# Second FFN products: a fifth tile by quarters in the second half of the columns, and another order of its tiles

## The chip, the cores and the metric

The kernel runs on one core of a Trainium2 chip. The metric is the time of one execution on the device in microseconds (us), the median of several runs. TensorE (PE) multiplies, VectorE (DVE), ScalarE (ACT) and GpSimd (POOL) prepare operands and take results away, and SyncE (SP) issues the transfers from the chip's main memory. Each engine works through its own list of instructions in order.

## What is computed

One decoder layer on 512 tokens of width 1024 in float32: a feed-forward network (FFN), a token mixer and a second FFN, each with a norm before and after it and a residual sum.

```python
def swiglu_ffn(x, w_in, w_out):
    gate, up = jnp.split(x @ w_in, 2, axis=-1)
    return (jax.nn.silu(gate) * up) @ w_out          # (512,1024) @ (1024,5632), then (512,2816) @ (2816,1024)

x = x + 0.5 * rms_norm(swiglu_ffn(rms_norm(x, g0), w_in1, w_out1), p0)
x = x + rms_norm(token_mixer(rms_norm(x, g1), ...), p1)
x = x + 0.5 * rms_norm(swiglu_ffn(rms_norm(x, g2), w_in2, w_out2), p2)
```

The change concerns the second product of both FFNs, h @ w_out, with h the gated 512 x 2816 array.

## The kernel before

**Split operands.** Every operand of a large product is kept as two arrays: a high part (ACT copies the value into TensorE's fast 32-bit format, lines 273 and 812) and a low part, the rest (DVE subtracts, lines 275 and 813). A product of two tiles is then three products: high by high, high by low, low by high.

**The second product by tiles.** `ffn_out` (line 858) works in two halves of the 1024 output columns. In each half it adds up 11 tiles; a tile (its number is called k2 in the code) is 256 of the 2816 inner positions. `OUT` (line 83) is the order of the tiles in each half. A whole tile (`plain`, line 886) takes 48 matrix multiplications of 128 x 256 (line 893). A tile by quarters (`quartered`, line 906) uses a scheme of Winograd's kind with seven instead of eight block products, and takes 42 (line 901). `QUARTERED` (line 82) names the tiles by quarters: six in the first half, four in the second. Their common results are put together once per half (`common`, lines 925 to 929) and added to the sums (`add`, line 934, its operations on line 863).

**What a tile by quarters needs beside that.** Its weights are split twice: three quarters as they are (128 x 768), and then, after four sums in place in the loaded buffer (`sum_quarters`, line 306), all four quarters (128 x 1024). On the side of h there are the quarters as they are (`h_quarters`, line 822, three of four) and four sums (`h_sums`, line 837, on DVE's line 844), which `s_tile` splits. The sums of h stay in place in `hf` if the tile is quartered in the second half too (`stay`), and the quarters are kept (`kept`) until then. Otherwise the sums go to a buffer of their own (`hsum`).

**Buffers.** Split weights have four places (`WBUF`), split h has three places under the tag "s" (`s_place`); two of the three hold tiles 9 and 10 (`AGAIN`) from the end of the first half until they are used in the second. `PLACES` and `LATER` put some parts of h into four buffers `xq` of the FFN's input that are free by then. Quarters with no place there go into "raw" buffers (named `once`), the ring of three through which weights of the first product and of the mixer are loaded. Weights of w_out are loaded by SP through the ring "raw2" of five buffers, in the order of `OUT`. The buffer "gpre" holds the gain of the norm before each part (line 152).

**The last four tiles of the second half** (`LAST`) are done in another order: their weights and h are all prepared, and `chunk` (line 984) goes through the four groups of 128 tokens, so that the first group's norm and residual sum start while the others are multiplied. `post1` (lines 485 and 493) does this, with the root taken on POOL (line 442).

**What follows the first FFN.** `head4` (line 548) starts the mixer's first four products (`head_mm`, line 543) while the norms of the last two groups of tokens are still made: `scaled` (line 465) writes the normed rows, `trans` turns them on TensorE (line 348).

**Order of work.** The source is written in the wished order. A scheduler that runs at build time, with an estimate of each instruction's duration, sets the order in which each engine's list is written, and when a buffer of a ring is handed on. Nothing is reordered at run time.

Of the kernel before, what the change touches and what calls it, by code (L numbers as in the profile page):

```python
# [9 lines left out]
F32R = mybir.dt.float32r  # L10
AF = mybir.ActivationFunctionType
ALU = mybir.AluOpType
PSUM = bass.MemoryType.PSUM

P = 128
T = 512
D = 1024
# [5 lines left out]
RAW, WBUF, PAD, LATE, NEXT, FRONT, STEP = 3, 4, 128, 112, 64, 96, 16  # L23
PAIRS = NF // 2
# [54 lines left out]

QUARTERED = [(2, 3, 4, 6, 7, 8), (2, 4, 6, 8)]
OUT = [list(range(PAIRS)), [9, 2, 4, 10, 6, 8, 0, 1, 3, 5, 7]]
LAST = 4
PLACES, LATER = {2: 1, 4: 2, 6: 0, 8: 3}, {0: (1, 0), 7: (2, 3)}

AGAIN, ROWS = (9, 10), (18, 19, 20, 21)

# [27 lines left out]
class Layer:  # L116
# [705 lines left out]
    def h_quarters(self, k2, n=None):  # L822

        src = self.by_chunk(k2)
        parts = self.x_place(n) if n is not None else [
            self.wp.tile([P, D], F32R, tag="raw", bufs=RAW, name=self.nm("once"))[:, P - 2 * STEP :] for _ in range(2)
        ]
        parts = [v[:, : 3 * QUARTER].rearrange("p (k c t) -> p k c t", c=2, t=P) for v in parts]
        self.two_parts(*(v[:, 0] for v in parts), src[:, 0, 1])
        self.two_parts(*(v[:, 1:] for v in parts), src[:, 1])  # L830
        return [[None] + [v[:, j] for j in range(3)] for v in parts]
# [5 lines left out]
    def h_sums(self, k2, stay):  # L837

        a = self.by_chunk(k2)
        f = self.hf[:, 2 * k2 : 2 * k2 + 2, :]  # L840
        if not stay:
            f = self.sp.tile([P, 2, T], F32, tag="xn", bufs=1, name=self.nm("hsum"))
        v = f.rearrange("p k (c u t) -> p k u c t", u=2, t=P)
        tt = lambda out, x, y, op: self.nc.vector.tensor_tensor(out, x, y, op=op)
        tt(v[:, 0, 0], a[:, 0, 1], a[:, 0, 0], ALU.subtract)
        tt(v[:, 1, 0], v[:, 0, 0], a[:, 1, 0], ALU.add)
        for k in range(2):
            tt(v[:, k, 1], a[:, k, 1], v[:, 1, 0], ALU.subtract)
        return f

    def s_tile(self, f):
# [6 lines left out]
    def ffn_out(self, gpost_row, scale, after, trans, head):  # L858
# [4 lines left out]
        tt = lambda out, a, b, op: nc.vector.tensor_tensor(out, a, b, op=op)  # L863
        seq = [(half, k2) for half in range(2) for k2 in OUT[half]]
        made = deque((h, None) for h in self.hs)
# [3 lines left out]
        def more(n):  # L869
            while count[0] < min(n, len(seq)):  # L870
                half, k2 = seq[count[0]]
                count[0] += 1
                if k2 in QUARTERED[half]:
                    if k2 not in kept:
                        stay = k2 in QUARTERED[1]
                        kept[k2] = self.h_quarters(k2, PLACES.get(k2)), self.h_sums(k2, stay)
                    a, f = kept[k2]
                    made.append((a, self.s_tile(f)))
                elif half and k2 in AGAIN:
                    made.append(again.popleft())  # L880
                else:
                    made.append((self.h_tile(k2, self.x_place(*LATER[k2]) if half and k2 in LATER else None), None))
                    if not half and k2 in AGAIN:
                        again.append(made[-1])
# [47 lines left out]
        def add(C, T, u):  # L932
            for v in range(2):
                tt(C[u][v], C[u][v], T[u, v], ALU.add)
# [9 lines left out]
        for half in range(2):  # L944
            C = [[self.ps() for _ in range(2)] for _ in range(2)]
            M, T, left = None, None, len(QUARTERED[half])
            for m, k2 in enumerate(OUT[half][: PAIRS - LAST * half]):
                more(n + 2)
# [9 lines left out]
                else:  # L958
                    w = self.pull()
                    more(len(seq) if half and m == PAIRS - LAST - 1 else n + 3)  # L960
                    for i in (0, 2, 1, 3):
# [13 lines left out]
        ws = []  # L975
        for k2 in OUT[1][-LAST:]:
            ws.append(self.pull())
            more(n + 1)
            n += 1
        hs = [made.popleft()[0] for _ in range(LAST)]  # L980

        add(C, T, 1)

        def chunk(i):
            vn = [(v, n) for v in range(2) for n in range(LAST)]
            if i == 0:

                vn.sort(key=lambda f: f[1])
            for v, n in vn:
                plain(C, ws[n], hs[n], i, v, False)  # L990
                if v and i == NT - 1:
                    self.drop(ws[n])
                if v and n == LAST - 1 and i == 0:
                    add(C, T, 0)
                if n == LAST - 1:
                    yield 2 - v
# [78 lines left out]
    def ffn_items(self, name, w_in, w_out):  # L1075
# [47 lines left out]
        for h in range(2):  # L1123
            for k2 in OUT[h]:
                src = w_out[k2 * 2 * P : (k2 + 1) * 2 * P, h * 512 : (h + 1) * 512].rearrange("(k p) d -> p k d", p=P)
                key = (name, "out", h, k2)
                made.append(Item(key, [Load(key, src, 2, 512, "raw2", 5, 8)], sums=k2 in QUARTERED[h]))
                if k2 in QUARTERED[h]:
                    made.append(Item(key, ()))
# [699 lines left out]
```

## Time and profile before

| | |
|---|---|
| median of 3 runs | 936.55 us (936.34 to 937.08) |
| the profiled execution | 936.35 us, its span 934.6 us, granted TensorE clock 0.998 |
| busy in the span | PE 926.2 us, weight loads 891.8, DVE 772.1, ACT 511.4, POOL 106.5 |
| second product of the first FFN | from 224.04 us to about 341.7 us |
| second product of the second FFN | from 812.82 us to the end |

Span is the time from the first to the last instruction; 1.75 us of the execution lie outside it. In a row of the timeline stand the start, the length of a run of like instructions, the engine, the line, the operation with output and inputs, and the count. In a group's row stand the count, the busy time and the mean duration of one. The granted clock is that which the chip gave TensorE, as a share of full speed.

### The profile page before, as it was taken

The page shows a single profiled execution, that of the slowest core. Times are in us where ns is not written, and L with a number is a line of the kernel's source. Part 1 is how long each engine was busy: PE and PEld are TensorE (multiplying, and loading weights), DVE is VectorE, ACT ScalarE, POOL GpSimd, SP SyncE. Part 2 cuts the span into 40 slices and gives each one's busy share as a digit, 9 for nine tenths or more (in the row PEclk, how much of TensorE's full clock was granted, in tenths as well). Part 3 has the DMA queues.
Part 4 walks back from the last instruction along what each step waited for, and adds up shares of the span by engine and source line. Part 5 has one row for each costly group of instructions (what it writes and reads, how often), then busy time and mean ns, then how long its engine had stood idle before and what let it go on. Part 6 is the DMA issues. An engine that isn't in the chain of part 4 may idle for free.

```text
span 934.6 us, 18052 instructions
## 1 busy us (share of the span) xinstructions
PE 926.2 (99%) x7471; PEld 891.8 (95%) x7471; DVE 772.1 (83%) x1044; ACT 511.4 (55%) x735; POOL 106.5 (11%) x172
## 2 busy tenths in 40 slices
PE   9999999999999999999999999999999999999997
PEld 7999999999999999998887887899999999999997
DVE  6899988889988877698766565799899889998884
ACT  7645454557456466956533445595454545655541
POOL 3530000000001045200010310313000000000101
PEclk9999999999999999999999999999999999999999
DMA  9253343332352025421212124352354435334212
GB/s 313 94 157 91 119 132 113 93 112 71 114 177 91 24 72 134 114 70 54 81 46 69 46 91 150 98 181 70 112 158 136 136 116 159 111 91 126 79 46 91
DMA packets 86956, 101.35 MB, mean 108 GB/s; under 512 B 4277, under 2 KB 66777, under 8 KB 86874
## 3 DMA queue, kind: packets, MB, share of 16 engines
q1 hardware_dynamic: 86586, 99.68, 34.9%
q8 instruction: 58, 0.95, 0.4%
q10 hardware_dynamic: 288, 0.52, 0.2%
q14 instruction: 24, 0.20, 0.1%
HBM read 98.10 MB, written 2.10 MB: 107 GB/s over the span
## 4 chain that ended last, share of the span: by engine, by line
PE 62%; ACT 1%; issue 0%; DVE 0%; POOL 0%; DVEq 0%; POOLq 0%; ACTq 0%
PE ps L603 22%; PE ps L893 7%; PE ps L533 6%; PE ps L901 5%; PE ps L179 5%; PE ps L181 5%; PE ps L180 5%; PE ps L1307 2%; PE ps L348 1%; PE ps L543 1%; PE ps L1488 0%; PE ps L1399 0%; PE ps L1600 0%; PE ps L1573 0%; PE ps L1353 0%; PE ps L1597 0%
## 5 line engine op out<-in xcount | busy, mean ns | idle before, releaser
L273 ACT CAST w<-raw 128x1024 fp32r<-128x1024 f32 (+1 forms) x238 | 244.4, 1035 | 231.7 <-PE ps L603 92.8
L275 DVE TENSOR_TENSOR w<-raw,w 128x1024 fp32r<-128x1024 f32 (+1 forms) x238 | 290.9, 1229 | 38.0 <-ACT w L273 37.5
L603 PE MATMUL ps<-xq,w 128*128 128x256 f32 x2016 | 237.1, 277 | 0.0
L603 PEld LDWEIGHTS ps<-xq,w 128*128 128x128 f32 x2016 | 232.9, 188 | 0.0
L603 PE MATMUL ps<-sq,w 128*128 128x256 f32 x1512 | 178.0, 276 | 0.3
L603 PEld LDWEIGHTS ps<-sq,w 128*128 128x128 f32 x1512 | 174.3, 188 | 1.1 <-ACT ps L654 0.9
L893 PE MATMUL ps<-w,hs 128*128 128x256 f32 x960 | 113.0, 276 | 0.0
L893 PEld LDWEIGHTS ps<-w,hs 128*128 128x128 f32 x960 | 110.7, 188 | 0.0
L289 DVE TENSOR_TENSOR raw<-raw,raw 128x1024 f32<-128x1024 f32 x72 | 89.8, 1251 | 8.3 <-DMA raw<-in_ffn_w_in_dram 6.7
L179 PE MATMUL ps<-w,xq 128*128 128x512 f32 x192 | 78.0, 407 | 0.1
L180 PE MATMUL ps<-w,xq 128*128 128x512 f32 x192 | 74.9, 391 | 0.0
L181 PE MATMUL ps<-w,xq 128*128 128x512 f32 x192 | 74.9, 392 | 0.0
L438 POOL TENSOR_SCALAR col<-col 128x1 f32<-128x1 f32 x24 | 8.3, 347 | 513.4 <-ACT junk L437 513.3
L901 PE MATMUL ps<-w,hs 128*128 128x256 f32 x480 | 57.7, 276 | 0.0
L901 PEld LDWEIGHTS ps<-w,hs 128*128 128x128 f32 x480 | 55.9, 188 | 0.0
L533 PE MATMUL ps<-xq,w 128*128 128x256 f32 x480 | 55.7, 278 | 0.0
L533 PEld LDWEIGHTS ps<-xq,w 128*128 128x128 f32 x480 | 54.9, 188 | 0.5 <-issue 0.5
L179 PEld LDWEIGHTS ps<-w,xq 128*128 128x128 f32 x192 | 36.1, 188 | 8.5 <-issue 0.9
L181 PEld LDWEIGHTS ps<-w,xq 128*128 128x128 f32 x192 | 36.0, 188 | 8.0 <-DVE xq L355 0.3
L812 ACT CAST hs<-hf 128x1024 fp32r<-128x1024 f32 x32 | 33.7, 1052 | 17.5 <-PE ps L901 10.8
L180 PEld LDWEIGHTS ps<-w,xq 128*128 128x128 f32 x192 | 36.1, 188 | 7.3 <-DVE w L281 0.3
L813 DVE TENSOR_TENSOR hs<-hf,hs 128x1024 fp32r<-128x1024 f32 x32 | 39.0, 1217 | 1.3 <-ACT hs L812 1.2
(259 smaller groups left out, 1136.8 us busy)
## 6 DMA issues: line engine op xcount, KB each, us to landing
raw<-in_ffn_w_in_dram SPq DMA_DIRECT2D x98, 512.0 KB, 3.7
raw<-in_ffn_w_out_dram SPq DMA_DIRECT2D x44, 512.0 KB, 4.3
raw<-in_w_mix_in_dram SPq DMA_DIRECT2D x28, 512.0 KB, 3.7
raw<-in_w_mix_out_dram SPq DMA_DIRECT2D x8, 512.0 KB, 3.9
out_dram<-xs SPq DMA_DIRECT2D x8, 256.0 KB, 2.0
xs<-in_x_dram SPq DMA_DIRECT2D x6, 256.0 KB, 4.5
gpost<-in_norm_post_dram SPq DMA_DIRECT2D x3, 512.0 KB, 3.6
gpre<-in_norm_pre_dram SPq DMA_DIRECT2D x2, 512.0 KB, 4.8
```

Of the source, the lines that this page charges most:

```text
L179: mm(ps, sh, mh, start=start, stop=False, **kw)
L180: mm(ps, sh, ml, start=False, stop=False, **kw)
L181: mm(ps, sl, mh, start=False, stop=stop, **kw)
L273: nc.scalar.copy(hi, raw)
L275: self.low = nc.vector.tensor_tensor(lo, raw, hi.bitcast(F32), op=ALU.subtract)
L289: (nc.vector if late else nc.gpsimd).tensor_tensor(o, o, c, op=ALU.add)
L533: mm(ps[:, u0:u1], w[:, a, k, :], self.xop(k, b, u0, u1), start=k + n + m == 0, stop=k == ND - 1 and n == 2, skip_group_check=True,)
L603: self.nc.tensor.matmul(ps[:, c], wb[b][:, k, v], left[d][:, k, :], start=first and a + n + k == 0, stop=n == 2 and k == KH - 1, skip_grou ...
L812: self.nc.scalar.copy(hi, src)
L813: self.nc.vector.tensor_tensor(lo, src, hi.bitcast(F32), op=ALU.subtract)
L893: mm(out, a[kk][:, i * P : (i + 1) * P], w[:, b, kk, QUARTER * v : QUARTER * (v + 1)], start=begin and c == kk == n == 0, stop=kk == 1 and ...
L901: mm(ps[:, QUARTER * c : QUARTER * (c + 1)], A[a][:, c], B[b], start=begin and c == n == 0, stop=n == 2, skip_group_check=True,)
```

## The change

Tile 3 is now done by quarters in the second half too, so it keeps its quarters in two raw buffers from the first half on, and its sums of h stay in place. Tile 7, quartered in the first half alone, finds one raw buffer and puts its other quarters into the buffer "gpre". The order of the second half is 9, 2, 4, 3, 6, 8, 10 and then the last four 0, 1, 7, 5 (before: 9, 2, 4, 10, 6, 8, 0 and 1, 3, 5, 7). Tile 0 takes its place for split h under the tag "s" and no longer in `xq`. In `h_sums` the last two subtractions of 128 x 256 become one of 128 x 512 with a repeated operand; that holds for every quartered tile.

```diff
-QUARTERED = [(2, 3, 4, 6, 7, 8), (2, 4, 6, 8)]
-OUT = [list(range(PAIRS)), [9, 2, 4, 10, 6, 8, 0, 1, 3, 5, 7]]
-LAST = 4
-PLACES, LATER = {2: 1, 4: 2, 6: 0, 8: 3}, {0: (1, 0), 7: (2, 3)}
+QUARTERED = [(2, 3, 4, 6, 7, 8), (2, 3, 4, 6, 8)]
+OUT = [list(range(PAIRS)), [9, 2, 4, 3, 6, 8, 10, 0, 1, 7, 5]]
+LAST, APART = 4, 7
+PLACES, LATER = {2: 1, 4: 2, 6: 0, 8: 3}, {7: (2, 3)}
...
-        parts = self.x_place(n) if n is not None else [
-            self.wp.tile([P, D], F32R, tag="raw", bufs=RAW, name=self.nm("once"))[:, P - 2 * STEP :] for _ in range(2)
-        ]
+        once = lambda pool, tag, bufs, o: pool.tile([P, D], F32R, tag=tag, bufs=bufs, name=self.nm("once"))[:, o:]
+        if n is not None:
+            parts = self.x_place(n)
+        else:
+            places = [(self.wp, "raw", RAW, P - 2 * STEP), (self.cp, "gpre", 1, STEP // 2)]
+            parts = [once(*places[k2 == APART and m]) for m in range(2)]
...
-        for k in range(2):
-            tt(v[:, k, 1], a[:, k, 1], v[:, 1, 0], ALU.subtract)
+        tt(v[:, :, 1], a[:, :, 1], v[:, 1:2, 0].broadcast_to([P, 2, 2, P]), ALU.subtract)
```

## The prediction

> **What bounds the kernel now.** I read the busy times first, then the windows of the second half of the columns in both FFNs, then the timelines of TensorE (PE) and VectorE (DVE) there, and last the waits behind the first FFN. The page:
>
> ```profile
> span 934.6 us, 18052 instructions
> ...
> PE 926.2 (99%) x7471; PEld 891.8 (95%) x7471; DVE 772.1 (83%) x1044; ACT 511.4 (55%) x735; POOL 106.5 (11%) x172
> ...
> L893 PE MATMUL ps<-w,hs 128*128 128x256 f32 x960 | 113.0, 276 | 0.0
> ```
>
> The windows from the start of the second half to the last four tiles, 35.36 us in each FFN; the columns are the window, its length, then busy time and count of PE, weight loads, DVE, ACT, POOL, the granted clock, DMA share and GB/s:
>
> ```profile
> 282.52:317.88 35.36, 35.36 (x315) 35.36 (x313) 31.70 (x44) 21.82 (x34) 2.25 (x7) 1.00 0.23 74
> 871.30:906.66 35.36, 35.36 (x314) 35.36 (x313) 31.69 (x44) 21.80 (x34) 2.25 (x7) 1.00 0.24 74
> ```
>
> PE is busy without a gap, at full clock. DVE is busy for 31.70 of 35.36 us, so PE bounds, with 3.66 us of DVE to spare. The PE timeline of the first FFN gives the price of a multiplication:
>
> ```profile
> 271.64 16.48 PE L893 MATMUL ps<-w,hs 128*128 128x256 f32 x144
> 287.96 1.52 PE L901 MATMUL ps<-w,xq 128*128 128x256 f32 x12
> ...
> 312.44 5.60 PE L893 MATMUL ps<-w,xq 128*128 128x256 f32 x48
> ...
> 317.88 4.24 PE L893 MATMUL ps<-w,hs 128*128 128x256 f32 x36
> ```
>
> From the first row's start to the second's lie 16.32 us and 144 multiplications, so they start 16.32/144 = 0.1133 us apart. The 276 ns of the group are one's time through the array, in which others start. A whole tile is 48 x 0.1133 = 5.44 us (312.44 to 317.88), a quartered one 42 x 0.1133 = 4.76.
>
> **The change part by part.**
>
> *Fewer multiplications.* Six per FFN, twelve in all: -12 x 0.1133 = **-1.36 us**, all on the bounding engine. Whether it stays depends on the rest.
>
> *DVE in the second half of the columns.* These are its rows in the first FFN, with two of the first half's first:
>
> ```profile
> 226.44 0.41 DVE L306 TENSOR_TENSOR raw<-raw 128x256 f32<-128x256 f32 x1
> 226.78 0.41 DVE L844 TENSOR_TENSOR hf<-hf 128x256 f32<-128x256 f32 x1
> ...
> 284.22 0.94 DVE L275 TENSOR_TENSOR w<-raw,w 128x768 fp32r<-128x768 f32 x1
> 285.09 2.38 DVE L475 TENSOR_TENSOR y<-ps,gpost 128x256 f32<-128x256 f32 x6
> ...
> 290.39 2.36 DVE L275 TENSOR_TENSOR w<-raw,w 128x1024 fp32r<-128x1024 f32 x2
> ...
> 294.47 0.95 DVE L275 TENSOR_TENSOR w<-raw,w 128x768 fp32r<-128x768 f32 x1
> 295.45 1.80 DVE L306 TENSOR_TENSOR raw<-raw 128x256 f32<-128x256 f32 x4
> 298.43 2.09 DVE L275 TENSOR_TENSOR w<-raw,w 128x1024 fp32r<-128x1024 f32 x2 [1.17 <-ACT w L273]
> ...
> 304.57 1.23 DVE L275 TENSOR_TENSOR w<-raw,w 128x1024 fp32r<-128x1024 f32 x1 [1.19 <-ACT w L273]
> ...
> 318.33 1.28 DVE L863 TENSOR_TENSOR ps<-ps,hf 128x512 f32<-128x512 f32 x2
> 319.52 1.21 DVE L275 TENSOR_TENSOR w<-raw,w 128x1024 fp32r<-128x1024 f32 x1
> ```
>
> What each takes until the next may start: a split of 1024 1.14 us (2.36 - 1.22 in the pair), of 768 0.87 (284.22 to 285.09) or 0.98 if the next needs its result (294.47 to 295.45); a sum of quarters 0.34 (226.44 to 226.78) or (1.80 - 0.42)/3 = 0.46 if the next sum needs it; an add of 512 0.60. From the last sum's end (295.45 + 1.80 = 297.25) to the second split that needs it, through ScalarE's (ACT's) cast, 298.43 - 297.25 = **1.18**; the row names that wait, 1.17. I call this the handover. Tile 3 now adds per FFN one split of 768 (0.87) and four sums (4 x 0.34 = 1.34): 31.70 + 2.21 = 33.9 us of a window that shrinks to 35.36 - 0.68 = 34.68. So the sum fits, by 0.8 us; the order decides. A quartered tile costs DVE 0.98 + 4 x 0.46 + 1.14 + 1.14 = 5.1 us with its sums back to back, more than its 4.76 on PE; a whole one 2.28 against 5.44. Before, whole tile 10 stood between the quartered ones; now 2, 4, 3, 6 and 8 follow one another.
>
> I stepped through DVE's list in the new built order with these prices. PE starts tile 2 at 287.96 as before, then 4 at 292.72, 3 at 297.48, 6 at 302.24, 8 at 307.00, 10 at 311.76, the last four at 317.20. The second weights of a quartered tile are needed 18 multiplications and one more place in, at its start + 2.04 + 0.11.
> - Tile 3: first split at 291.53, three sums from 292.51, a split of h, the fourth sum at 294.91; 295.33 + 1.18 = second split at 296.51, done about 297.7. Needed 299.6.
> - Tile 6: first split 297.65, sums from 298.63 with a split of h (1.14) after the first, the last ends 301.45; tile 8's first split fills the handover; second split 302.63, done 303.8. Needed 304.4.
> - Tile 8: sums from 303.77, again with a split of h between, the last ends 306.59; tile 10's split fills the handover; second split 307.77, done 308.95. Needed 309.15: **0.2 us of spare**.
>
> So no wait there, by a hair. Then DVE makes the splits and four adds of the last four tiles. Their fourth tile, 5, finds a place for h and for weights only when tile 10 ends, at 317.20. The ACT cast of the same kind before:
>
> ```profile
> 318.08 1.05 ACT L273 CAST w<-raw 128x1024 fp32r<-128x1024 f32 x1 [4.06 <-PE ps L893]
> ```
>
> It starts 0.2 after PE's release at 317.88. Now ACT casts h at 317.4 and the weights at 318.35; DVE comes to the h of tile 5 at 319.35, behind the adds, to its weights at 320.49, done 321.6. The first group of tokens needs them 36 multiplications and one after 317.20, at 321.39. Before: 319.52 + 1.21 = 320.73 against 322.07, a spare of 1.3. I cost the difference at 0.2 to 0.3 us per FFN, **+0.6** for two. The bounds: 0 if DVE is slightly earlier than stepped; 1.2 each if one more operation of 1.14 slips ahead of it. The price lies nearest to the stepped one.
>
> [...]
>
> *Last differences of h.* One of 512 in place of two of 256, twelve times. Two take at least 2 x 0.34; one of 512, by the adds, 0.60. So each saves 0.08 or a little more, up to 1 us if all of it were on the path. But it lies beside the first product and the first half, where PE is the bound as well: I take 0. Tile 7's sums also stand earlier in DVE's list and two of tile 3's later, all still beside the first product; 0, or one sum of 0.34 at most if PE came to wait there.
>
> *Places.* Loads of w_out take:
>
> ```profile
> raw<-in_ffn_w_out_dram SPq DMA_DIRECT2D x44, 512.0 KB, 4.3
> ```
>
> Tile 7's quarters lie in the buffer of the gain until PE has used them in the first half; in the first FFN the gain's load now stands on SP's queue behind that release and behind some 18 w_out loads. Its reader is the normed row of the first group of tokens, after the last four tiles have begun: 0. Two mixer loads now wait on SP for tile 3's raw buffers, until 302.24 in the steps above; the w_out loads of tiles 7 and 5 queue behind them, land about 306.5 to 308, and have their first readers on DVE at 314.67 and 320.49 (on ACT about 1.2 earlier): 0, and up to 4.3 us if that cover of some 5 us were gone.
>
> *Behind the first FFN.* The build moves one instruction: the second group of head products is fed by two splits of mixer weights on DVE, and the normed row of the third group of tokens (line 465), which stood ahead of the last group's line 485 and 493, now stands behind them.
>
> ```profile
> 342.88 0.75 DVE L465 SCALAR_TENSOR_TENSOR xn<-xs,col,gpre 128x512 f32<-128x512 f32 x1
> 343.56 0.41 DVE L485 TENSOR_TENSOR hf<-ps,gpost 128x256 f32<-128x256 f32 x1
> 344.08 0.75 DVE L493 SCALAR_TENSOR_TENSOR xs<-y,col,xs 128x512 f32<-128x512 f32 x1
> 344.75 0.74 DVE L493 SCALAR_TENSOR_TENSOR xs<-hf,col,xs 128x512 f32<-128x512 f32 x1
> 345.41 1.22 DVE L275 TENSOR_TENSOR w<-raw,w 128x1024 fp32r<-128x1024 f32 x1
> ```
>
> What gates line 493 is GpSimd's (POOL's) root, and what follows the split is the waiting PE:
>
> ```profile
> 343.18 0.86 POOL L442 TENSOR_TENSOR col<-col,nhalf 128x1 f32<-128x1 f32 x1
> ```
>
> ```profile
> PEld ps L543 <- DVE w L275: 0.3, 1, 0.3
> ```
>
> The root ends at 344.04, line 493 starts at 344.08 and cannot start earlier; the row of 0.67 us (342.88 to 343.56) that lay in that time now comes after, so the split starts at 346.08 instead of 345.41, and PE, which waits 0.3 for it already, waits 0.67 more: **+0.67**. Bounds: 0 if the estimate of the order of arrival is off, 1.4 if both normed rows of the pair end up there.
>
> **Sum.** -1.36 + 0.6 + 0.67 = -0.1 us against the profiled execution (span 934.6 and 1.75 outside it, 936.35 us; the median of the runs, 936.55, is 0.2 above). **Forecast 936.4 us**; 0.2%, or 1.87 us, is about what a measurement can tell from no change.
>
> **Rivals.**
> 1. *The saving stays.* The last tile is in time and line 465 costs nothing: 936.55 - 1.36 = 935.2; with only one of the two, 935.8. For it: 83% of DVE's time, and a miss of the last tile by 0.2 is within my stepping's error. Against it: the wait for line 275 is there already. Chance 0.22.
> 2. *DVE is late from tile 8 on: slower.* Tile 8's second weights have 0.2 us. One handover that is not filled there (tile 10's split not ready to fill it) puts DVE 1.18 late; PE stands still 1.18 - 0.2 = 1.0 per FFN, and the last tile moves with it: -1.36 + 2 x 1.0 + 2 x 0.3 + 0.67 = +1.9, 938.4. Two such: +1.9 + 2 x 1.18 = +4.3, 940.8. It decides as soon as tile 8's second split ends after 309.15. For it: rows show both handovers of the window unfilled (1.17, 1.19). Against it: the new order has something to put in each. [...] Chance 0.24, half of it beyond 938.4.
> 3. *A multiplication's 276 ns were the price*: -12 x 0.276 = -3.3, 933.2 or, with the costs, 934.5. Against it: the 0.1133 between starts. Chance 0.04.
>
> **How the numbers follow.** My forecast, within 0.6 us, has 0.50, the three rivals 0.22, 0.24 and 0.04. The range from 935.0 to 938.5 holds the forecast, rival 1 and one handover per FFN; outside are the two-handover slip (0.13) and rival 3 (0.04). Faster by over 0.2% (below 934.7): 0.05. Slower by over 0.2% (above 938.4): 0.17. Within: 0.78.
>
> **What would show it.** Tiles 2 to 8 without a gap on PE, starts 4.76 apart; the last four from 317.20; a gap of 0.2 to 0.3 at about 321.4 that ends with line 275; a wait of the head products for line 275 of 0.9 to 1.0 instead of 0.3; the same in the second FFN, but for the head. A gap of 0.5 or more ahead of the last four, or PE's busy time unchanged, would make it wrong.

## The result, and the profile after

| | before | after |
|---|---|---|
| median | 936.61 us (6 runs, 936.05 to 937.94) | 941.08 us (6 runs, 940.33 to 941.47) |
| ratio, 95% interval | | 1.0044 (1.0032 to 1.0057) |
| the profiled execution | 936.35 us, span 934.6 | 940.33 us, span 938.2 |

The change made the kernel 4.5 us slower. The forecast was 936.4, the range ended at 938.5, and beyond that end lay only the second rival in its larger form (940.8 with two handovers lost per FFN). The profiled executions differ by 4.0 us, since the one after is the fastest of its six. Of these, 3.6 us lie in the spans; another 0.4 lies outside the span (2.13 us there instead of 1.75) and stays unexplained.

The page of the changed kernel:

```profile
span 938.2 us, 18025 instructions
...
PE 928.0 (99%) x7459; PEld 892.0 (95%) x7459; DVE 775.1 (83%) x1042; ACT 510.6 (54%) x737; POOL 104.8 (11%) x172
```

Twelve multiplications fewer, and PE busy 1.8 us longer: a share of 99% tells nothing here. The windows of the second half, from its start to the last four tiles, do:

```profile
282.63:318.62 35.99, 35.24 (x309) 34.85 (x308) 33.55 (x50) 21.95 (x36) 2.44 (x8) 1.00 0.36 103
873.32:909.32 36.00, 35.54 (x309) 35.15 (x308) 33.83 (x51) 22.09 (x36) 2.44 (x8) 1.00 0.24 74
```

They should have shrunk from 35.36 to 34.68 us and grew to 36.0. PE is no longer busy throughout. VectorE's load is what was forecast (33.55 and 33.83 against 33.9), and it is not full. TensorE's timeline shows where it waits; lines of the new kernel are two higher. First FFN:

```profile
266.74 1.52 PE L903 MATMUL ps<-w,xq 128*128 128x256 f32 x12
...
271.75 16.48 PE L895 MATMUL ps<-w,hs 128*128 128x256 f32 x144
288.07 1.52 PE L903 MATMUL ps<-w,xq 128*128 128x256 f32 x12
...
303.71 0.96 PE L903 MATMUL ps<-w,hs 128*128 128x256 f32 x7
305.40 2.21 PE L903 MATMUL ps<-w,hs 128*128 128x256 f32 x17 [0.73 <-DVE w L275]
...
309.49 3.17 PE L903 MATMUL ps<-w,hs 128*128 128x256 f32 x24
...
313.18 8.32 PE L895 MATMUL ps<-w,hs 128*128 128x256 f32 x72
```

The last quartered tile of the first half takes 271.75 - 266.74 = 5.01 us instead of 4.76: **0.25** of waiting. The five of the second half take 313.18 - 288.07 = 25.11 instead of 5 x 4.76 = 23.80: **1.31**, in tile 6 (the row at 305.40 names the second split of the weights, line 275; its 0.73 counts from the end of the multiplication before, and by the usual spacing the row was due 0.90 earlier, at 303.71 + 7 x 0.1133 = 304.50) and tile 8 (24 in 3.17 us instead of 2.88). Second FFN:

```profile
857.21 1.52 PE L903 MATMUL ps<-w,xq 128*128 128x256 f32 x12
...
862.44 16.48 PE L895 MATMUL ps<-w,hs 128*128 128x256 f32 x144
878.76 1.52 PE L903 MATMUL ps<-w,xq 128*128 128x256 f32 x12
...
895.78 2.20 PE L903 MATMUL ps<-w,hs 128*128 128x256 f32 x17 [0.42 <-DVE w L275]
...
899.86 3.26 PE L903 MATMUL ps<-w,hs 128*128 128x256 f32 x24
...
903.66 8.64 PE L895 MATMUL ps<-w,hs 128*128 128x256 f32 x72
```

The same places: 5.23 - 4.76 = **0.47**, and 24.90 - 23.80 = **1.10**. Something new stands in the last row: 72 multiplications in 8.64 us are (8.64 - 0.276)/71 = 0.1178 us apart, where the same row of the first FFN (8.32) has 0.1133. It stays so to the end of the kernel; 240 multiplications at 0.0045 us more are **1.07 us**.

Behind the first FFN, first after, then before:

```profile
342.94 4.82 PE L543 MATMUL ps<-xq,w 128*128 128x256 f32 x40
348.21 1.19 PE L543 MATMUL ps<-xq,w 128*128 128x256 f32 x8 [0.45 <-DVE w L275]
...
356.56 32.80 PE L533 MATMUL ps<-xq,w 128*128 128x256 f32 x288
```

```profile
341.76 6.13 PE L543 MATMUL ps<-xq,w 128*128 128x256 f32 x48
...
355.05 32.80 PE L533 MATMUL ps<-xq,w 128*128 128x256 f32 x288
```

From the head products to line 533 it takes 13.62 us instead of 13.29: **0.33**. From tile 10's start to the head products it takes 342.94 - 313.18 = 29.76, before (312.44 to 341.76) 29.32, for the same 240 multiplications: **0.44**, the last tile. The row of that wait and the one ahead of it:

```profile
322.70 0.28 PE L895 MATMUL ps<-w,hs 128*128 128x256 f32 x1
323.13 2.89 PE L895 MATMUL ps<-w,hs 128*128 128x256 f32 x23 [0.15 <-DVE w L275]
```

The 23 multiplications behind the wait take 2.89 us, where 22 x 0.1133 + 0.276 = 2.77; the 17 at 305.40 and at 895.78 take 2.21 and 2.20, where 16 x 0.1133 + 0.276 = 2.09. These three waits cost 0.11 to 0.12 us more than themselves, which the differences above include.

Now VectorE, in the first half. These are two second splits of weights, after:

```profile
245.34 0.42 DVE L306 TENSOR_TENSOR raw<-raw 128x256 f32<-128x256 f32 x1
246.95 2.36 DVE L275 TENSOR_TENSOR w<-raw,w 128x1024 fp32r<-128x1024 f32 x2 [1.20 <-ACT w L273]
...
251.35 1.81 DVE L306 TENSOR_TENSOR raw<-raw 128x256 f32<-128x256 f32 x4
254.35 2.09 DVE L275 TENSOR_TENSOR w<-raw,w 128x1024 fp32r<-128x1024 f32 x2 [1.20 <-ACT w L273]
...
289.03 1.80 DVE L306 TENSOR_TENSOR raw<-raw 128x256 f32<-128x256 f32 x4
```

And the same before:

```profile
245.05 0.88 DVE L306 TENSOR_TENSOR raw<-raw 128x256 f32<-128x256 f32 x2
245.85 2.43 DVE L275 TENSOR_TENSOR w<-raw,w 128x1024 fp32r<-128x1024 f32 x2
...
252.72 1.22 DVE L813 TENSOR_TENSOR hs<-hsum,hs 128x1024 fp32r<-128x1024 f32 x1
253.98 2.09 DVE L275 TENSOR_TENSOR w<-raw,w 128x1024 fp32r<-128x1024 f32 x2
...
287.38 1.79 DVE L306 TENSOR_TENSOR raw<-raw 128x256 f32<-128x256 f32 x4
```

Before, another split stood between the last sum and the second split that needs it (a whole tile's weights at 245.85, a split of h at 252.72), and VectorE went on without a pause. After, nothing stands there, and it waits 1.20 us for ScalarE's cast, at tiles 4 and 6 of each FFN. From 224 us to the half it waits 2.3 us more for such casts (6.6 instead of 4.3; some of these handovers stood open before as well) and works 0.7 us less. So it reaches the first sums of the second half (line 306) at 289.03 instead of 287.38, 1.65 us late (1.54 against TensorE, whose tile 2 starts 0.11 later), before the fifth tile has begun. The prediction started its steps from the rows of before at just this place. From there on its steps hold, moved by that lateness. It had the second splits of tiles 3 and 6 at 296.51 and 302.63; they start 1.55 and 1.49 us later:

```profile
298.06 2.09 DVE L275 TENSOR_TENSOR w<-raw,w 128x1024 fp32r<-128x1024 f32 x2 [1.17 <-ACT w L273]
...
304.12 1.23 DVE L275 TENSOR_TENSOR w<-raw,w 128x1024 fp32r<-128x1024 f32 x1 [0.25 <-ACT w L273]
```

### The profile page after: what moved, and what is told of

It reads as the page before. It is cut to its first block, busy times and chain, and to the rows that moved or that the text cites. A ratio compares the mean times of both kernels' runs of the same rounds, so it can differ in the third digit from the quotient of the medians.

```text
span 938.2 us, 18025 instructions
## 1 busy us (share of the span) xinstructions
PE 928.0 (99%) x7459; PEld 892.0 (95%) x7459; DVE 775.1 (83%) x1042; ACT 510.6 (54%) x737; POOL 104.8 (11%) x172
## 5 line engine op out<-in xcount | busy, mean ns | idle before, releaser
L895 PE MATMUL ps<-w,hs 128*128 128x256 f32 x960 | 114.4, 277 | 0.2 <-DVE w L275 0.2
L895 PEld LDWEIGHTS ps<-w,hs 128*128 128x128 f32 x960 | 111.7, 188 | 0.4 <-DVE w L275 0.4
L903 PE MATMUL ps<-w,hs 128*128 128x256 f32 x528 | 65.1, 277 | 1.4 <-DVE w L275 1.3
L903 PEld LDWEIGHTS ps<-w,hs 128*128 128x128 f32 x528 | 62.0, 188 | 2.6 <-DVE w L275 2.6
L812 ACT CAST hs<-hf 128x1024 fp32r<-128x1024 f32 x36 | 37.8, 1049 | 13.6 <-PE ps L895 8.4
L813 DVE TENSOR_TENSOR hs<-hf,hs 128x1024 fp32r<-128x1024 f32 x36 | 43.8, 1217 | 0.0
```

The source lines that it names most:

```text
L812: self.nc.scalar.copy(hi, src)
L813: self.nc.vector.tensor_tensor(lo, src, hi.bitcast(F32), op=ALU.subtract)
L895: mm(out, a[kk][:, i * P : (i + 1) * P], w[:, b, kk, QUARTER * v : QUARTER * (v + 1)], start=begin and c == kk == n == 0, stop=kk == 1 and ...
L903: mm(ps[:, QUARTER * c : QUARTER * (c + 1)], A[a][:, c], B[b], start=begin and c == n == 0, stop=n == 2, skip_group_check=True,)
```

## The experiments

Theory A: the change opened handovers in VectorE's list, so VectorE is late, and the waits are that lateness. Theory B: four more quartered tiles in a row are too much for VectorE from wherever they start. Ratios are against runs of the kernel before on the same chip.

**1. Less to do between the halves.** This version of the changed kernel leaves out four of the eight products with the gain, so its result is not the layer's.

```diff
-    def post0(self, pieces, g, scale):
+    def post0(self, pieces, g, scale, times=1):
-        y, parts = self.st("y"), []
+        y, parts = self.st("y") if times else g[:, :512], []
...
-            self.nc.vector.tensor_tensor(y[:, v], ps, g[:, v], op=ALU.mult)
+            for _ in range(times):
+                self.nc.vector.tensor_tensor(y[:, v], ps, g[:, v], op=ALU.mult)
...
-                ys = [self.post0(pieces(C, i), g, scale) for i in range(NT)]
+                ys = [self.post0(pieces(C, i), g, scale, int(i < 2)) for i in range(NT)]
```

> The changed kernel without four of the eight products with the gain between the halves (line 475, groups 2 and 3 of the tokens; the residual sum reads the gain in their place), which takes 4 x 0.39 = 1.57 us from VectorE at 283 to 289 us and leaves the rest of its list as it is. Theory A, VectorE comes out of the first half 1.65 us late and that lateness is what runs out into the waits of tiles 6 and 8: both waits (1.31 us in the first FFN, 1.10 in the second) go, 941.1 - 2.4 = 938.7 us, those of the last tile and of the first half stay. Theory B, the run of four quartered tiles after tile 2 is too much for VectorE whatever it starts from: no wait goes, 941.0 +- 0.3.

Measured: 938.59 us, ratio 1.0020 (1.0009 to 1.0031). Its first sums of the second half, in VectorE's timeline:

```profile
287.40 1.79 DVE L306 TENSOR_TENSOR raw<-raw 128x256 f32<-128x256 f32 x4
```

They stand where they stood before the change, and the waits of tiles 6 and 8 are 0.15 us in the first FFN and none in the second. That is theory A's number, and B falls: the same run of five quartered tiles runs through, but for these 0.15 us, when VectorE starts it 1.6 us earlier. The last tile still waits, 0.42 and 0.30 us.

**2. Lateness given to the kernel before** (the same switch in the kernel before, with `1 + (i > 1)` in place of `int(i < 2)`).

> The kernel before with the same four products with the gain done twice, 1.57 us more on VectorE between the halves in each FFN. Theory A: the kernel before has the spare that the changed one lacks, only the last tile's 1.3 us are overdrawn, 936.6 + 2 x (0 to 0.3), 936.6 to 937.2 us. Theory B, VectorE is near its bound in any case and each us on it goes to the end: 936.6 + 3.1 = 939.7.

Measured: 937.07, ratio 1.0002 (0.9993 to 1.0012). VectorE comes to the first sums of the second half 1.0 us later against TensorE than in the kernel before (in the first FFN at 289.36, where tile 2 starts at 288.90), less than the 1.57 us put in and than the 1.54 of the changed kernel. TensorE has no wait on VectorE in the second products. The kernel before has room for 1.0 us; the changed one has used it up.

**3. The order of the tiles alone.**

```diff
-OUT = [list(range(PAIRS)), [9, 2, 4, 10, 6, 8, 0, 1, 3, 5, 7]]
+OUT = [list(range(PAIRS)), [9, 2, 4, 3, 6, 8, 10, 0, 1, 5, 7]]
-PLACES, LATER = {2: 1, 4: 2, 6: 0, 8: 3}, {0: (1, 0), 7: (2, 3)}
+PLACES, LATER = {2: 1, 4: 2, 6: 0, 8: 3}, {7: (2, 3)}
```

> The kernel before with the new order of the tiles (9, 2, 4, 3, 6, 8, 10, then 0, 1, 5, 7), tile 3 still whole in the second half. Its list on VectorE in the first half is that of the kernel before. Theory A: no lateness out of the first half, no wait of tiles 6 and 8; only the tail of the order can cost, 0 to 0.3 per FFN and up to 0.7 behind the first FFN: 936.6 to 937.6. Theory C, the order alone makes the waits (tiles 9 and 10 hold two of three places for split h to the last): 939 or more.

Measured: 936.93, ratio 0.9999 (0.9990 to 1.0007), no wait on VectorE in the second products. This order costs nothing, and theory C falls. It ends with 5, 7 as before; the changed kernel ends with 7, 5, and that swap wasn't tried alone.

**4. The differences of h as before** (in the changed kernel, `h_sums` with its loop over two operations of 256).

> The changed kernel with the last two differences of h of 256 each again, as before. Theory A: the unfilled waits of the first half stand in its list as well, so nothing changes: 941.1 +- 0.5. Theory D, the one operation of 512 moved the list and is the cause: back to 936.5.

Measured: 941.71, ratio 1.0048 (1.0034 to 1.0061). The merged operation is not the cause. By elimination (order but for that swap, merge) the two handovers probably come from what the fifth tile needs in the first half: tile 3's quarters and sums are kept, tile 7's quarters lie in another place, and the splits of both stand elsewhere in the list. Which of these the planner (the scheduler at build time) answered to wasn't tried alone, so why the list changed stays open.

**5. The handovers filled.** In the changed kernel the split of the next h is held behind the four sums, and the second split of the weights behind that:

```diff
@@ feed @@
-            for _ in self.split():
-                pass
+            self.qfinish()
+            second = self.qhalf
+            g = self.split()
+            next(g)
+            if second:
+                self.qopen = g
+            else:
+                for _ in g:
+                    pass
@@ s_tile @@
-        self.two_parts(*parts, f)
+        lo = self.two_parts(*parts, f, *[self.qsum] * bool(self.qopen))
+        self.qfinish(lo)
@@ ffn_out @@
+                self.feed()
                 more(n + 2)
```

The edit has beside these the lines that set `qhalf` and `qsum`, `qfinish` itself, and its calls in `split` and `pull`. `next(g)` issues the cast of a second split; its VectorE part waits in `qopen` until `qfinish` issues it behind `lo`. `qsum` is the last of the four sums.

> The changed kernel with another order on VectorE alone, by emission: of a quartered tile the four sums come first, then the split of the next h (held behind the last sum), then the second split of the weights (held behind that of h), so that the split of h fills the handover where it stood between the sums before. It fills one of the two handovers that the change opened in the first half and three in the second. Theory A (unfilled handovers make VectorE late): VectorE is 1.1 us or more earlier at the half, the waits of tiles 6 and 8 shrink to less than half, 941.1 - 1.5 to - 3.5 us: 937.6 to 939.6. Theory B (the sum of the work on VectorE in the run of quartered tiles is too much, 5.1 us a tile against 4.76): the handover filled is lost again in sums that wait on each other, 941.1 +- 0.7.

Measured: 936.13, ratio 0.9988 (0.9979 to 0.9997). VectorE's timeline in the first and in the second half:

```profile
242.47 1.80 DVE L309 TENSOR_TENSOR raw<-raw 128x256 f32<-128x256 f32 x4
244.19 2.35 DVE L834 TENSOR_TENSOR hs<-hf,hs 128x1024 fp32r<-128x1024 f32 x2
246.46 2.35 DVE L278 TENSOR_TENSOR w<-raw,w 128x1024 fp32r<-128x1024 f32 x2
...
292.70 1.80 DVE L309 TENSOR_TENSOR raw<-raw 128x256 f32<-128x256 f32 x4
294.42 1.22 DVE L834 TENSOR_TENSOR hs<-hf,hs 128x1024 fp32r<-128x1024 f32 x1
295.67 2.09 DVE L278 TENSOR_TENSOR w<-raw,w 128x1024 fp32r<-128x1024 f32 x2
```

The split of h (line 834 here) stands in the handover. Of the two handovers that the change opened in the first half, that of tile 4 is filled and that of tile 6 still open (1.19 us at 253.85). TensorE has no wait on VectorE left in either second product, the last tile included, and the slow spacing is gone. That is 5 us below the changed kernel with the same operations, and below theory A's range, which had left the waits of the first half and the slow spacing in. It is also the first version below the kernel before: against that kernel's profile the two second products are 0.66 and 0.68 us shorter, nearly the whole saving of 12 x 0.1133, and the step behind the first FFN is 0.35 longer. Run once more beside the changed kernel, the two gave:

> The changed kernel with the filled order in both halves once more: no wait of TensorE on VectorE in either second product, no slow stretch, 5 us below the changed kernel on the same chip and 0.5 to 1.2 us below the kernel before (ratio 0.9987 to 0.9995).

> The changed kernel once more, on the chip on which the filled order runs beside it. Time 941.1 +- 0.5. Its waits come from the order on VectorE, which is built in, so they stand at the same tiles with the same lengths within 0.1 us. Open is the slow stretch (0.1178 us between multiplications instead of 0.1133): if it is a property of the place, it starts at 900 us again and nowhere else; if a wait sets it off by chance, it may start at another of the waits or not at all, and the time differs by 0.0045 us for each multiplication in it.

Measured: 935.87, ratio 0.9990 (0.9981 to 0.9999), and 941.29, ratio 1.0046 (1.0034 to 1.0059). The changed kernel's waits stood at the same tiles (0.73 at tile 6 of the first FFN and 0.44 of the second), but the slow spacing stood elsewhere: not in the second products, but from 774 to 794 us in the first product of the second FFN, where it takes 0.7 us:

```profile
788.62 2.99 PE L603 MATMUL ps<-sq,w 128*128 128x256 f32 x24
```

In the second product the wait of the last tile of the second FFN, hidden by the slow spacing the first time (TensorE was 0.5 us behind by then), shows instead (0.42 us).

**6. The same order in the kernel before.**

> The same order in the kernel before, which has no wait of TensorE on VectorE in its second products. Theory A and B alike: nothing to gain, 936.8 +- 0.4. If it gains, VectorE's order costs something there that the trace of before did not show.

Measured: 937.92, ratio 1.0008 (1.0000 to 1.0017). Nothing gained, perhaps 0.8 us lost: the median lies 0.7 above the expected range. Its profile doesn't show where, being of an execution of 936.59 us, one of its fastest. In these two kernels the order is worth something only in the one where VectorE is late.

**7. One half at a time.** The switch of experiment 5 in the first or in the second half of the columns only.

> The changed kernel with the filled order of VectorE in the first half of the columns alone. Theory A1, the cause is the lateness out of the first half: VectorE is some 1.4 us earlier at the half, the waits of the first half (0.25 and 0.47 us) and those of tiles 6 and 8 (1.31 and 1.10) go, and the slow stretch behind them (1.07): 941.1 - 3.1 to - 4.2 = 936.9 to 938.0. Theory A2, the unfilled handover of tile 3 in the second half is the cause: less than 1.5 us gained, 939.6 or more.

> The changed kernel with the filled order of VectorE in the second half of the columns alone; VectorE still comes out of the first half 1.65 us late, and the waits of the first half stay. Theory A1, that lateness is the cause: the one handover of tile 3 that is now filled gives back at most 1.1 us per FFN and its sums cost 0.1 each, so half of the waits of tiles 6 and 8 stays: 938.7 to 940. Theory A2, the handover of the second half is the cause: those waits go, 941.1 - 2.4 - 1.1 = 937.6 or less.

Measured: first half 938.48, ratio 1.0017 (1.0008 to 1.0025); second half 939.38, ratio 1.0024 (1.0015 to 1.0032). By the times the second stands in theory A1's range and the first 0.5 us above its own. The first has no wait on VectorE in the first half; tiles 2 to 8 take 23.90 and 24.17 us instead of 23.80, with short waits at tile 8, and the slow spacing, which A1 had gone, takes 1.65 us of its profile, most of it from tile 8 of the second FFN to the end, as in this row:

```profile
901.28 8.64 PE L917 MATMUL ps<-w,hs 128*128 128x256 f32 x72
```

In the trace of the second, though, the waits of tiles 6 and 8 are gone in both FFNs, as A2 says: in the second FFN tiles 2 to 8 take 23.80 us although VectorE comes to its first sums 0.68 us after tile 2 begins (880.76 against 880.08), as late as in the changed kernel (879.42 against 878.76). What costs there is the spacing, over nearly the whole second half of the first FFN (TensorE's timeline, and the window with the granted clock as the third column from the end):

```profile
272.49 17.12 PE L917 MATMUL ps<-w,hs 128*128 128x256 f32 x144
```

```profile
272.49:338.00 65.51, 65.51 (x559) 65.51 (x558) 55.88 (x82) 33.55 (x64) 7.60 (x22) 1.00 0.32 98
```

So neither A1 nor A2 is the whole cause: the lateness out of the first half and tile 3's own unfilled handover together overdrew the room, and taking away either one removes the waits of tiles 6 and 8, all but the short ones named. The last tile's wait stayed in both (0.41 us in the first FFN of the first version, 0.73 in the second FFN of the second) and is gone only when both halves are filled.

**8. The step behind the first FFN** (experiment 5, and `scaled(2, 0)` not held behind the first split of mixer weights).

> The filled order in both halves, and behind the first FFN the normed row of the third group of tokens (line 465) ahead of the first split of mixer weights, so that it lies in the time in which line 493 waits for GpSimd's root, as before the change. The prediction's step, 0.67 us for this move: 936.1 - 0.7 = 935.4. The profile of the changed kernel, where the stretch from the head products to line 533 is 13.62 us against 13.29 before: 0.33, 935.8; the times cannot tell these apart, the profile's stretch can (13.29 or 12.95).

Measured: 936.59, ratio 0.9993 (0.9985 to 1.0002), no difference from experiment 5 that the times can show. From the head products to line 533 its profile has 13.38 us; experiment 5 has 13.64, the kernel before 13.29. The move costs 0.3 us by the profiles, half of what was forecast.

**9. A wait put into the kernel before.**

> The kernel before with the products with the gain of groups 2 and 3 done four times instead of once between the halves of the second FFN alone: 12 x 0.39 = 4.7 us more on VectorE there. By the prices of the prediction the second weights of tile 8 have 4.0 us of spare and the last tile 1.3, so TensorE waits some 0.7 us at tile 8 and about 2.7 more at the last tile: 936.8 + 3.4 = 940.2. Open beside that: in the changed kernel the multiplications after two waits of the second FFN start 0.1178 us apart to the end instead of 0.1133. If a wait at this place is what makes them so, the same spacing shows here behind the wait of tile 8 and adds about 200 x 0.0045 = 0.9 us: 941.1. If it comes from something else in the changed kernel, the spacing stays 0.1133.

Measured: 939.23, ratio 1.0018 (1.0007 to 1.0028). Its first wait came earlier than expected, at tile 2: its row names the delayed products with the gain (line 476) and 0.19 us. TensorE's timeline:

```profile
878.35 1.65 PE L902 MATMUL ps<-w,xq 128*128 128x256 f32 x12 [0.19 <-DVE y L476]
879.84 2.99 PE L902 MATMUL ps<-w,hs 128*128 128x256 f32 x24
```

24 in 2.99 us are 0.1180 apart: the slow spacing begins at a wait of 0.19 us in a kernel that has none of the change in it. Here it ended after some 10 us. The median fell 1 us short of the expected 940.2, and not by the path foreseen: neither tile 8 nor the last tile waits, and the built list of VectorE differs there too (a split of h and splits of weights stand between the sums of tile 2). In this profile the second product is 0.9 us longer than before, by the wait at tile 2 and the spacing; the rest of the 2.3 us between the medians is not located.

## Why the prediction was wrong

| term, both FFNs | predicted | profile after |
|---|---|---|
| twelve multiplications | -1.36 | -1.36 (by count) |
| first half of the columns | 0 | +0.25 + 0.47 |
| tiles 3, 6 and 8 | 0 (spare 0.2) | +1.31 + 1.10 |
| last tile | +0.6 | +0.44, and in the second FFN hidden |
| behind the first FFN | +0.67 | +0.33 |
| slow spacing after waits | not foreseen | +1.07 |
| the remainder | 0 | -0.05 |
| sum (span) | -0.1 | +3.6 |

- *What bounds, and the price of a multiplication*: right. The 0.1133 us hold in the rows before any wait, and the version without waits has 1.34 of the 1.36 in its second products.
- *VectorE's load*: right, 33.55 and 33.83 us against 33.9, though in a window that grew to 36.0. (Four sums at 0.34 are 1.36, not 1.34; that changes nothing.)
- *"PE starts tile 2 at 287.96 as before"*, and VectorE's list from there with the rows of before: **the step that failed.** The steps took VectorE's position at the half from the old trace; the list of the first half was not stepped. Of the moved operations the prediction wrote "all still beside the first product; 0, or one sum of 0.34 at most". It costed the operations, not the places of the others around them: two splits that had stood in handovers stood elsewhere in the new list, and two handovers of 1.18 (measured 1.20) opened. VectorE came to the second half 1.54 us late against TensorE. With the prediction's own spare of 0.6 us at tile 6 that makes a wait of 0.94, and the profile has 0.90; the unfilled handover of tile 3, the other half of the cause by experiment 7, was already in its steps.
- *The rivals*: the second had the mechanism and the price of an unfilled handover, but looked for it at tile 8 and gave two of them 0.13. That its size fits (+4.3 forecast, +4.5 measured) is in part luck: 1.07 us of slow spacing and 0.4 outside the span, which it did not know, are in the measured sum.
- *The last tile*: foreseen, and too small: 0.44 in the first FFN against 0.2 to 0.3. The lateness isn't needed for it (0.42 and 0.30 in experiment 1); 0.12 of it lies behind the wait, in 23 multiplications that take 2.89 us instead of 2.77, which the steps did not count.
- *Line 465*: right in kind, half in size. "Cannot start earlier" was wrong of line 493: it starts 2.00 us after the head products (344.94 in the row below the list, less 342.94), where it was 2.32 (344.08 - 341.76). GpSimd's root took 0.55 us instead of 0.86; why isn't shown.
- *Differences of h, order, loads*: right; experiments 3 and 4 show no cost, and in the profile after no engine waits for a transfer in either second product. What the new places did to the list wasn't tried alone.

```profile
344.94 0.75 DVE L493 SCALAR_TENSOR_TENSOR xs<-y,col,xs 128x512 f32<-128x512 f32 x1 [0.46 <-POOL col L442]
```

## What to carry to other kernels

An operation that moves may have been the filler of another's wait, and a list has to be stepped from the first place where it differs, not from where the change's own work begins. Here VectorE, busy for 33.55 of 35.99 us, fed the bounding engine, and its order decided more than its load: the same operations took 941.1 or 936.1 us, depending on what stood in a 1.2 us handover. Put the wait's filler there by name, rather than leave it to a planner's estimates.

## What the runs showed of the hardware

In seven of the fourteen profiles TensorE's multiplications of 128 x 256 go 0.1178 us apart instead of 0.1133, 4% slower, for some 10 us (experiment 9) to 67 us (experiment 7), at a granted clock of 1.00 (the windows from 904 to 928 us in the changed kernel's first profile and from 272.49 to 338 us in experiment 7). Each such stretch begins right behind an interruption of TensorE's stream that cost from some 0.2 us (experiment 3, whose row of 24 at its start takes 3.09 us instead of 2.88) to 0.73 us (experiment 7), and most interruptions are followed by none: of seven waits in the second products of the changed kernel's first profile only the last is. Such a stretch does not need the change: experiment 3 has one of 30 us in the first product of the first FFN, which the edit leaves alone.

```profile
52.62 14.30 PE L603 MATMUL ps<-sq,w 128*128 128x256 f32 x120
```

In the changed kernel one profile has it at the end of the second FFN and another, with the same waits, has it in an earlier product. In the first it cost 1.07 us, more than the interruption it follows: the row of 24 at 899.86 takes 3.26 us instead of 2.88. What sets it off and what ends it stays open.
